# Gate and value projections: two sums of weight blocks formed by accumulating transfers from GpSimd's queue

## The chip, the core and the metric

One core of a Trainium2 chip runs the whole program. The metric is device time in microseconds, the median of the runs shown. Engines are named as in the profile: PE is TensorE (PEld its weight loads), DVE is VectorE, ACT is ScalarE, POOL is GpSimd, SP is SyncE, which issues nearly all transfers.

## The reference, cut to what matters

One layer of a hybrid trunk is followed by a gated feed-forward block. The part that the change touches is the pair of wide products `h @ w_gate` and `h @ w_val`: 512 tokens, 2048 inputs, 5504 outputs each, in float32.

```python
h = rmsnorm(x, norm_ffn_g[l])
gate = causal_dwconv(h @ w_gate[l], f_conv_w[l], f_conv_b[l])   # taps over 3 tokens
val = h @ w_val[l]
x = x + (jax.nn.gelu(gate) * val) @ w_down[l]
```

## The kernel before

Everything lies with channels on the 128 partitions and the 512 tokens along the row. The gate and value products ("gv") are 43 passes, of which each makes two 128-wide tiles of gate outputs or of value outputs in turn (the last pass takes one of each), and a pass is two stages, so there are 86 stages `s`, each for one half of the inputs. A stage uses a fast 2x2 block scheme with seven products in place of eight: from four weight blocks W0..W3 of 128x512 it needs seven operands, namely W1, W2, W3 and four sums. In the raw area of the stage, seven blocks of 512 columns, the transfer puts W0..W3 in blocks 0 to 3; `b_adds` then makes block 4 = W0+W1 and block 5 = W0+W2 in one DVE instruction of 1024 columns (L1147), block 6 = block 4 + W2 (L1148) and block 0 = block 6 + W3 (L1149). Blocks 4 and 5 are the sums that the change calls S1 and S3.

Each operand is split into a rounded part and its remainder so that three products give nearly full precision: `b_cast` copies all seven blocks (3584 columns) on ACT into the high area (L1153), `b_sub` subtracts that from the raw area on DVE into the low area (L1157), and `b_mm` (L208 to L210) runs 84 matmuls of 128x256 on PE, three for each of 28 weight tiles, the third of the three with the low part. There are two raw areas (`aR0`, `aR1`), two high and two low ones, used by even and odd stages.

The order on each engine is the order in which the loop writes the instructions. In step `s` it writes: the transfer for stage `s+2` (it goes into the raw area that `b_sub(s)` has read, so SP waits for that instruction), stores of finished hidden tiles to `hidd` (two of 256 KB in every fourth step), the cast of stage `s+1`; in even steps the six instructions of `b_post` on DVE, which empty the banks of the pass before (L1191 to L1196), and a scaling (gate, L1204) or product (value, L1226); then the subtraction of `s+1`, the 84 matmuls of `s`, the sums of `s+2`, and for gate the taps (L1218).

The first two stages are prepared during the last 16 products of the block before ("wm", loop over `m`): the transfer of stage 0 is written at m = 10, its sums at m = 12, its cast and the transfer of stage 1 at m = 14. In that loop GpSimd adds squares into `x2` (L1262), once for each m. In the gv stages GpSimd has nothing to do.

Of the kernel before, what the change touches and what calls it, by code (L numbers as in the profile page):

```python
# [14 lines left out]
MUL, ADD, SUB, MAX, MIN = ALU.mult, ALU.add, ALU.subtract, ALU.max, ALU.min  # L15

P = 128
T = 512
# [30 lines left out]
def f(ap):  # L49
    return ap.bitcast(F32)  # L50
# [3 lines left out]
def trunk(ctx: ExitStack, tc: tile.TileContext, A: dict, out: bass.AP):  # L54
    nc = tc.nc
    V, S, G, PE = nc.vector, nc.scalar, nc.gpsimd, nc.tensor
# [15 lines left out]
    def pair(i, dt):  # L72
        return sl.tile([P, 2 * T], dt, tag=f"p{i}", name=f"p{i}")

    def part(t, i, n=1):
        return t[:, i * T:(i + n) * T]
# [9 lines left out]
    def slot(dt=F32, name="s"):  # L86
        q = mosubs if name in ("MOh", "MOl") else () if name == "acc" else subs[dt]
        if q:
            t = q.popleft()
            owner[id(t)] = (q, t)  # L90
        else:
            i = free.popleft()
            cnt[0] += 1
            t = sl.tile([P, T], dt, tag=f"s{i}", name=f"{name}_{cnt[0]}")
            owner[id(t)] = (i, t)
        return t

    def drop(*ts):
        for t in ts:
            i = owner.pop(id(t))[0]  # L100
            if isinstance(i, int):
                free.append(i)
            else:
                i.append(t)

    def acc_ps(name):
        return ps.tile([P, T], F32, tag="acc", name=name, bufs=5)
# [22 lines left out]
    def vcol(n, i=0, w=1):  # L130
        c = VCOL[n] + i
        return vec[:, c:c + w]
# [79 lines left out]
    def dense(pt, nch, xh, xl):  # L212

        for c in range(nch):
            wh, wl = wget()
            for k in range(8):
                i = c * 8 + k
                w = slice(k * P, (k + 1) * P)
                mm3(pt, wh[:, w], wl[:, w], xh[i], xl[i], i == 0, i == nch * 8 - 1)
            if c < nch - 1:  # L220
                pump()
# [768 lines left out]
    for k in range(KT):  # L990
        if k < 2 or k % 2 == 0:
            wh, wl = ready.popleft()
        w = slice(0, T) if k < 2 else slice((k % 2) * T, (k % 2) * T + T)
# [4 lines left out]
        for j in range(4):  # L998
            if k < 14:
                mm3(upt[j], xh[k][:, j::4], xl[k][:, j::4], wh[:, w], wl[:, w], k == 0, False)  # L1000
            elif k == 15:
                for q in range(14, 16):
                    w = slice((q % 2) * T, (q % 2) * T + T)
# [24 lines left out]
    for c in range(8):  # L1028
        wh, wl = wget()
        for j in range(4):  # L1030
            for q in range(2):
                k = 2 * c + q
                w = slice(q * T, (q + 1) * T)
# [78 lines left out]
    RS = [aR0, aR1]  # L1112
# [6 lines left out]
    def t_build(kp):  # L1119

        x = (p1 if kp % 2 else p0).rearrange("p (b t) -> p b t", t=HT)
        v = p2.rearrange("p (b t) -> p b t", t=HT)
        V.tensor_tensor(out=v[:, 0:2], in0=x[:, 0:1].to_broadcast([P, 2, HT]), in1=x[:, 1:3], op=SUB)
        V.tensor_tensor(out=v[:, 2], in0=x[:, 2], in1=v[:, 0], op=SUB)
        V.tensor_tensor(out=v[:, 3], in0=x[:, 3], in1=v[:, 2], op=SUB)
        if kp % 2 == 0:
            TP["half"] = [slot(F32R, "T") for _ in range(2)]
            TS[kp // 4].extend(TP["half"])
        h, l = [t[:, kp % 2 * HT:kp % 2 * HT + HT] for t in TP["half"]]
        split(h, l, x[:, 1])  # L1130
        TP[kp, 1] = h, l
        for src, qs in ((x[:, 2:4], (6, 2)), (v[:, 0:2], (3, 4)), (v[:, 2:4], (5, 0))):
            h, l = slot(F32R, "T"), slot(F32R, "T")
            TS[kp // 4].extend([h, l])
            split(h, l, src.rearrange("p b t -> p (b t)"))
            for j, q in enumerate(qs):
                TP[kp, q] = [t[:, j * HT:j * HT + HT] for t in (h, l)]

    def b_dma(s):
        if s < NS:  # L1140
            nc.sync.dma_start(out=RS[s % 2][:, 0:4 * T], in_=A["wgv"][s // 2, s % 2])

    def b_adds(s):
        if s >= NS:
            return
        v = RS[s % 2].rearrange("p (b t) -> p b t", t=T)
        V.tensor_tensor(out=v[:, 4:6], in0=v[:, 0:1].to_broadcast([P, 2, T]), in1=v[:, 1:3], op=ADD)  # L1147
        V.tensor_tensor(out=v[:, 6], in0=v[:, 4], in1=v[:, 2], op=ADD)  # L1148
        V.tensor_tensor(out=v[:, 0], in0=v[:, 6], in1=v[:, 3], op=ADD)  # L1149

    def b_cast(s, lo=0, hi=7):
        if s < NS:
            S.copy(out=part(RH[s % 2], lo, hi - lo), in_=part(RS[s % 2], lo, hi - lo))  # L1153

    def b_sub(s, lo=0, hi=7):
        if s < NS:
            V.tensor_tensor(out=part(RL[s % 2], lo, hi - lo), in0=part(RS[s % 2], lo, hi - lo),  # L1157
                            in1=f(part(RH[s % 2], lo, hi - lo)), op=SUB)
# [73 lines left out]
    def put_out():  # L1232
        while stores:
            o, i_ = stores.popleft()
            nc.sync.dma_start(out=o, in_=i_)
# [3 lines left out]
    for m in range(16):  # L1239
        pt = acc_ps("wm")  # L1240
        dense(pt, 1, MOh, MOl)
        put_out()
        if m > 0:
            drop(acc[m - 1])
        V.tensor_tensor(out=acc[m], in0=acc[m], in1=pt, op=ADD)
        stores.append((x1d[m], acc[m]))
        if m == 10:
            b_dma(0)
        elif m == 12:
            b_adds(0)  # L1250
        elif m == 14:
            assert not raws
            b_cast(0)
            b_dma(1)
        x = p1 if m // 2 % 2 else p0
        S.activation(out=part(x, m % 2), in_=acc[m], func=AF.Copy, scale=vcol("g_ffn", m))
        if m == 0:
            S.activation(out=x2, in_=acc[m], func=AF.Square)
        else:
            sq = slot(name="sq")  # L1260
            S.activation(out=sq, in_=acc[m], func=AF.Square)
            G.tensor_tensor(out=x2, in0=x2, in1=sq, op=ADD)  # L1262
            drop(sq)
        if m == 14:
            b_sub(0, 1, 4)
        elif m % 2 and m < 15:
            t_build(m // 2)
    drop(*MOh, *MOl)
# [2 lines left out]
    put_out()  # L1271
    t_build(7)
    b_adds(1)
    US = slot(name="u")

# [63 lines left out]
    for s in range(NS + 1):  # L1339
# [4 lines left out]
        if s < NS - 2:  # L1344
            b_dma(s + 2)
# [14 lines left out]
        if s < NS:  # L1360
            b_mm(s)
        b_adds(s + 2)
        if even and gate:
            g_taps(k0, n)
# [29 lines left out]
    for k in range(KD):  # L1394
        d_dma(k + 2)
        d_split(k + 1)
        if k == 6:
# [4 lines left out]
            for i in (1, 2):  # L1402
                t = pair(i, F32R)
# [230 lines left out]
```

## Time and profile before

| | us |
|---|---|
| median of 3 runs (2117.73 to 2120.08) | 2118.34 |
| the profiled execution's own time | 2120.67 |
| its span | 2118.9 |
| gv stages, first matmul to last | 738.1 to 1624.3 |
| PE, DVE, ACT, POOL busy, share of the span | 98, 71, 38, 14% |

Busy time of PE is made of matmuls that overlap, so 98% doesn't say that none of them waited. A short wait between two matmuls is seen only in their start times: in the gv stages these lie 0.12 us apart where nothing holds PE.

### The profile page before, as it was taken

Reading aid. Unit: us, or ns where it says so; the run is one execution under the profiler, and the core shown is the slowest. Engines: PE = TensorE matmul, PEld = TensorE weight load, DVE = VectorE, ACT = ScalarE, POOL = GpSimd, SP = SyncE. Lnnn points to the kernel's source line nnn. Section 1 sums busy time; section 2 is a strip of 40 time slices with the busy share of each in tenths; the row PEclk is TensorE's granted clock in tenths of the full one; section 3 lists DMA queues with packets and bytes.
Section 4 is the critical chain, followed back from the end, with each engine's and each line's share of the span. In section 5 each row is a group of like instructions: output and inputs, shape, how many; then the busy total and the mean of one; then the engine's idle time right before and its main releaser. Section 6 shows DMA issues by size and latency. Waiting matters only on the chain.

```text
span 2118.9 us, 31328 instructions
## 1 busy us (share of the span) xinstructions
PE 2067.7 (98%) x12956; PEld 1881.7 (89%) x12956; DVE 1507.2 (71%) x2017; ACT 799.2 (38%) x946; POOL 290.0 (14%) x511
## 2 busy tenths in 40 slices
PE   8999989999999999999999999999999999999997
PEld 7887778888888799999999999999998888888887
DVE  7699996458655788989889898898886544222235
ACT  5244433345424543333443334333343432111124
POOL 4877660001101200000000000000000000000003
PEclk9999999999999989999999999999999999999999
DMA  4222113222333323333433333333332555333352
GB/s 172 83 73 76 63 53 110 82 87 80 115 139 115 136 103 119 111 110 114 135 110 110 120 120 119 120 110 111 118 131 90 188 174 190 110 110 113 119 199 80
DMA packets 75369, 244.73 MB, mean 115 GB/s; under 512 B 8397, under 2 KB 14029, under 8 KB 64217
## 3 DMA queue, kind: packets, MB, share of 16 engines
q1 hardware_dynamic: 75224, 242.72, 33.5%
q8 instruction: 101, 1.65, 0.3%
q14 instruction: 44, 0.35, 0.0%
HBM read 220.12 MB, written 22.57 MB: 115 GB/s over the span
## 4 chain that ended last, share of the span: by engine, by line
PE 80%; DVE 13%; POOL 2%; issue 2%; ACT 2%; DMA 1%; SPq 0%; DVEq 0%; ACTq 0%; POOLq 0%
PE gv L210 14%; PE gv L208 14%; PE gv L209 13%; PE down L209 7%; PE down L210 7%; PE down L208 7%; DVE a L116 2%; PE o L208 1%; PE ws L208 1%; PE ws L210 1%; PE o L210 1%; PE o L209 1%; PE ws L209 1%; PE v L208 1%; PE v L210 1%
## 5 line engine op out<-in xcount | busy, mean ns | idle before, releaser
L210 PE MATMUL gv<-T,a 128*128 128x256 f32 x2408 | 687.2, 285 | 4.4 <-DVE a L1157 4.4
L208 PE MATMUL gv<-T,a 128*128 128x256 f32 x2408 | 683.7, 284 | 4.0 <-ACT a L1153 4.0
L209 PE MATMUL gv<-T,a 128*128 128x256 f32 x2408 | 683.0, 284 | 0.0
L210 PEld LDWEIGHTS gv<-T,a 128*128 128x128 f32 x2408 | 463.9, 193 | 9.6 <-DVE a L1157 4.9
L208 PEld LDWEIGHTS gv<-T,a 128*128 128x128 f32 x2408 | 464.1, 193 | 4.5 <-ACT a L1153 4.5
L1153 ACT CAST a<-a 128x3584 fp32r<-128x3584 f32 x86 | 274.8, 3196 | 502.9 <-DVE a L1149 373.1
L209 PEld LDWEIGHTS gv<-T,a 128*128 128x128 f32 x2408 | 464.1, 193 | 0.0
L116 DVE TENSOR_TENSOR a<-a,a 128x1024 fp32r<-128x1024 f32 (+2 forms) x205 | 238.6, 1166 | 302.1 <-ACT a L115 301.1
L1157 DVE TENSOR_TENSOR a<-a,a 128x3584 fp32r<-128x3584 f32 (+2 forms) x88 | 336.2, 3822 | 82.7 <-ACT a L1153 82.6
L115 ACT CAST a<-a 128x1024 fp32r<-128x1024 f32 (+2 forms) x205 | 198.7, 973 | 379.6 <-PE down L209 296.1
L1486 POOL TENSOR_TENSOR c<-c,c 128x256 f32<-128x256 f32 x24 | 17.8, 741 | 1339.3 <-ACT c L1484 1338.4
L208 PE MATMUL down<-c,a 128*128 128x512 f32 x448 | 175.4, 392 | 4.0 <-ACT c L115 4.0
L210 PE MATMUL down<-c,a 128*128 128x512 f32 x448 | 175.0, 391 | 0.0
L209 PE MATMUL down<-c,a 128*128 128x512 f32 x416 | 162.9, 392 | 0.1
L1147 DVE TENSOR_TENSOR a<-a 128x1024 f32<-128x1024 f32 x86 | 104.8, 1219 | 0.0
L208 PEld LDWEIGHTS down<-c,a 128*128 128x128 f32 x448 | 84.6, 189 | 22.1 <-ACT c L115 4.4
L210 PEld LDWEIGHTS down<-c,a 128*128 128x128 f32 x448 | 84.7, 189 | 17.6
L209 PEld LDWEIGHTS down<-c,a 128*128 128x128 f32 x416 | 78.6, 189 | 16.9 <-DVE c L116 0.7
L209 PE MATMUL down<-a,a 128*128 128x512 f32 x176 | 68.5, 389 | 0.0
L208 PE MATMUL down<-a,a 128*128 128x512 f32 x176 | 68.5, 389 | 0.0
L1218 DVE SCALAR_TENSOR_TENSOR p<-p,vec,p 128x511 f32<-128x511 f32 x86 | 62.5, 748 | 2.5 <-ACT p L1211 0.9
L1149 DVE TENSOR_TENSOR a<-a 128x512 f32<-128x512 f32 x86 | 60.5, 703 | 2.9
(589 smaller groups left out, 3608.1 us busy)
## 6 DMA issues: line engine op xcount, KB each, us to landing
a<-in_wgv SPq DMA_DIRECT2D x86, 1024.0 KB, 4.8
a<-in_wdB SPq DMA_DIRECT2D x55, 512.0 KB, 3.4
a<-in_wdA SPq DMA_DIRECT2D x40, 320.0 KB, 3.2
hidd<-p SPq DMA_DIRECT2D x40, 256.0 KB, 6.2
a<-in_wxm SPq DMA_DIRECT2D x16, 512.0 KB, 3.3
a<-in_wv SPq DMA_DIRECT2D x16, 512.0 KB, 3.2
a<-in_wo SPq DMA_DIRECT2D x16, 512.0 KB, 3.2
a<-in_wouts SPq DMA_DIRECT2D x16, 512.0 KB, 3.5
```

The costliest lines, as they stand in the source:

```text
L115: S.copy(out=h, in_=src)
L116: V.tensor_tensor(out=l, in0=src, in1=f(h), op=SUB)
L208: PE.matmul(pt, lhsT=wh, rhs=xh, start=first, stop=False)
L209: PE.matmul(pt, lhsT=wh, rhs=xl, start=False, stop=False)
L210: PE.matmul(pt, lhsT=wl, rhs=xh, start=False, stop=last)
L1147: V.tensor_tensor(out=v[:, 4:6], in0=v[:, 0:1].to_broadcast([P, 2, T]), in1=v[:, 1:3], op=ADD)
L1149: V.tensor_tensor(out=v[:, 0], in0=v[:, 6], in1=v[:, 3], op=ADD)
L1153: S.copy(out=part(RH[s % 2], lo, hi - lo), in_=part(RS[s % 2], lo, hi - lo))
L1157: V.tensor_tensor(out=part(RL[s % 2], lo, hi - lo), in0=part(RS[s % 2], lo, hi - lo), in1=f(part(RH[s % 2], lo, hi - lo)), op=SUB)
L1218: V.scalar_tensor_tensor(out=y1[:, s:], in0=gs[:, 0:T - s], scalar=vcol("f_cw", 3 * (k0 + j) + 2 - s), in1=y1[:, s:], op0=MUL, op1=ADD)
L1486: G.tensor_tensor(out=x2, in0=x2, in1=sq[:, 0:HT], op=ADD)
```

## The change

The transfer of a stage becomes three. SP's first puts W0 twice, into blocks 4 and 5 (512 KB); its second puts W1..W3 into blocks 1 to 3 (768 KB); block 0 is no longer loaded. A transfer on GpSimd's queue then adds W1 and W2, read from HBM again (512 KB), onto blocks 4 and 5. The DVE instruction L1147 is gone from all 86 stages. In the loop over m the transfers of stage 1 are written after the first part of the subtraction of stage 0, in place of right after its cast.

```diff
     def b_dma(s):
         if s < NS:
-            nc.sync.dma_start(out=RS[s % 2][:, 0:4 * T], in_=A["wgv"][s // 2, s % 2])
+            r, w = RS[s % 2], A["wgv"][s // 2, s % 2]
+            v = r.rearrange("p (b t) -> p b t", t=T)
+            nc.sync.dma_start(out=v[:, 4:6], in_=w[:, 0:T].unsqueeze(1).to_broadcast([P, 2, T]))
+            nc.sync.dma_start(out=r[:, T:4 * T], in_=w[:, T:4 * T])
+            nc.gpsimd.dma_start(out=r[:, 4 * T:6 * T], in_=w[:, T:3 * T], accum_op=ADD)
 
     def b_adds(s):
...
-        V.tensor_tensor(out=v[:, 4:6], in0=v[:, 0:1].to_broadcast([P, 2, T]), in1=v[:, 1:3], op=ADD)
         V.tensor_tensor(out=v[:, 6], in0=v[:, 4], in1=v[:, 2], op=ADD)
         V.tensor_tensor(out=v[:, 0], in0=v[:, 6], in1=v[:, 3], op=ADD)
...
         elif m == 14:
             assert not raws
             b_cast(0)
-            b_dma(1)
...
         if m == 14:
             b_sub(0, 1, 4)
+            b_dma(1)
```

On DVE, a value step and the step after it, in the kernel before (`a_73` and `a_68` are the raw areas, `a_72`/`a_70` the high ones, `a_69`/`a_71` the low ones):

```order
L1226 TENSOR_TENSOR p_76<-p_76,p_75 128x1024
L1157 TENSOR_TENSOR a_71<-a_68,a_70 128x3584
L1147 TENSOR_TENSOR a_73<-a_73 128x1024
L1148 TENSOR_TENSOR a_73<-a_73 128x512
L1149 TENSOR_TENSOR a_73<-a_73 128x512
L1157 TENSOR_TENSOR a_69<-a_73,a_72 128x3584
```

The same place now; line numbers are three higher:

```order
L1229 TENSOR_TENSOR p_76<-p_76,p_75 128x1024
L1160 TENSOR_TENSOR a_71<-a_68,a_70 128x3584
L1151 TENSOR_TENSOR a_73<-a_73 128x512
L1152 TENSOR_TENSOR a_73<-a_73 128x512
L1160 TENSOR_TENSOR a_69<-a_73,a_72 128x3584
```

The instruction of 1024 columns between a subtraction and the two sums of 512 columns is gone; nothing else on DVE moved.

On GpSimd's queue, the end of the loop over m and the first gv stages, in the changed kernel, with the semaphores that each row waits for (DMAHW is a transfer from SP, DMASW one from GpSimd):

```order
L1264 TENSOR_TENSOR x_360_5404<-x_360_5404,sq_6038 128x512 [waits Activation_49,Pool_49]
L1145 DMA a_68<-in_wgv 128x1024 [waits DMAHW6_49,DMAHW2_49,DVE_49]
L1264 TENSOR_TENSOR x_360_5404<-x_360_5404,sq_6073 128x512 [waits Activation_49]
L1145 DMA a_73<-in_wgv 128x1024 [waits DMAHW6_49,DMASW0_49,DVE_49]
L1145 DMA a_68<-in_wgv 128x1024 [waits DMAHW0_49,DMASW1_49,DVE_49]
```

The accumulating transfer of stage 1 stands between the additions of squares of m = 14 and m = 15, and from there on the queue holds only such transfers, each of which waits for SP's transfer of W0 into the same area.

## Rows read from the trace of the kernel before

**Rows 1.** Page part 4: chain of waits, share of the span by engine.

```profile
PE 80%; DVE 13%; POOL 2%; issue 2%; ACT 2%; DMA 1%; SPq 0%; DVEq 0%; ACTq 0%; POOLq 0%
```

**Rows 2.** Busy time of each engine in four stretches; first row names the columns.

```profile
core 0: us, PE busy (x) PEld busy (x) DVE busy (x) ACT busy (x) POOL busy (x), PEclk, DMA share, GB/s
746.00:786.00 40.00, 35.22 (x270) 34.84 (x269) 33.09 (x46) 15.45 (x9) 0.00 (x0) 0.87 0.28 103
786.00:900.00 114.00, 114.00 (x952) 114.00 (x951) 100.38 (x95) 45.64 (x28) 0.00 (x0) 1.00 0.35 116
1100.00:1300.00 200.00, 200.00 (x1653) 198.66 (x1652) 176.66 (x165) 76.96 (x45) 0.00 (x0) 1.00 0.35 114
1207.50:1214.00 6.50, 6.50 (x55) 6.49 (x55) 3.04 (x4) 3.46 (x2) 0.00 (x0) 1.00 0.79 241
```

**Rows 3.** Timeline of PE: start, us, engine, line, operation, at two stage starts.

```profile
922.40 0.28 PE L209 MATMUL gv<-T,a 128*128 128x256 f32 x1
922.62 0.39 PE L210 MATMUL gv<-T,a 128*128 128x256 f32 x1
...
1207.30 0.28 PE L209 MATMUL gv<-T,a 128*128 128x256 f32 x1
1207.51 0.39 PE L210 MATMUL gv<-T,a 128*128 128x256 f32 x1
```

**Rows 4.** Timeline of DVE and ACT over two stages; idle before in brackets.

```profile
1203.58 3.88 DVE L1157 TENSOR_TENSOR a<-a,a 128x3584 fp32r<-128x3584 f32 x1
1207.38 1.22 DVE L1147 TENSOR_TENSOR a<-a 128x1024 f32<-128x1024 f32 x1
...
1210.21 3.20 ACT L1153 CAST a<-a 128x3584 fp32r<-128x3584 f32 x1 [7.36 <-DVE a L1149]
...
1213.44 3.90 DVE L1157 TENSOR_TENSOR a<-a,a 128x3584 fp32r<-128x3584 f32 x1 [3.39 <-ACT a L1153]
1217.25 1.22 DVE L1147 TENSOR_TENSOR a<-a 128x1024 f32<-128x1024 f32 x1
1218.50 0.69 DVE L1148 TENSOR_TENSOR a<-a 128x512 f32<-128x512 f32 x1
...
1223.92 3.88 DVE L1157 TENSOR_TENSOR a<-a,a 128x3584 fp32r<-128x3584 f32 x1
```

**Rows 5.** Timeline of DVE: the subtractions of stages 3 and 85.

```profile
776.24 3.88 DVE L1157 TENSOR_TENSOR a<-a,a 128x3584 fp32r<-128x3584 f32 x1
...
1610.53 3.88 DVE L1157 TENSOR_TENSOR a<-a,a 128x3584 fp32r<-128x3584 f32 x1
```

**Rows 6.** Groups of instructions: the one that the change removes.

```profile
L1147 DVE TENSOR_TENSOR a<-a 128x1024 f32<-128x1024 f32 x86 | 104.8, 1219 | 0.0
```

**Rows 7.** Timeline at the start of the gv stages: POOL, DVE, ACT, PE.

```profile
739.30 1.64 POOL L1262 TENSOR_TENSOR x<-x,sq 128x512 f32<-128x512 f32 x1 [5.76 <-ACT sq L1261]
...
747.83 1.22 DVE L1147 TENSOR_TENSOR a<-a 128x1024 f32<-128x1024 f32 x1
...
750.54 3.18 ACT L1153 CAST a<-a 128x3584 fp32r<-128x3584 f32 x1 [4.06 <-DVE a L1149]
...
757.70 0.58 PE L210 MATMUL gv<-T,a 128*128 128x256 f32 x1 [3.13 <-DVE a L1157]
```

**Rows 8.** Transfers: issues (KB, median us to landing), and those of L1141 alone.

```profile
a<-in_wgv SPq DMA_DIRECT2D x86, 1024.0 KB, 4.8
...
a<-in_wxm SPq DMA_DIRECT2D x16, 512.0 KB, 3.3
...
L1141 SPq DMA_DIRECT2D a<-in_wgv x86: 327/332/425, 706.9 to 1594.1; - x86
...
DMA to landing us min/median/max: 4.6/4.8/7.2
```

**Rows 9.** Timeline: a GpSimd and a DVE instruction side by side.

```profile
726.95 1.59 POOL L1262 TENSOR_TENSOR x<-x,sq 128x512 f32<-128x512 f32 x1 [6.04 <-ACT sq L1261]
...
727.43 1.67 DVE L1149 TENSOR_TENSOR a<-a 128x512 f32<-128x512 f32 x1
```

## The prediction

> **What bounds the kernel now.** I read the chain of waits first: PE holds 80% of it and DVE 13% [rows 1], so a gain has to shorten PE's own time or a wait of PE. The stretches come next [rows 2]. From 786 to 900 us PE runs 952 matmuls in 114.0 us, 0.1197 us each; from 1100 to 1300 us it runs 1653 in 200.0 us, 0.1210 us each, at the same granted clock of 1.00. Something takes about 1% from PE in the later stretch although its busy time reads 200.00 of 200.00. DVE is busy 88% in both, which alone would not make it a suspect.
>
> The starts of the matmuls show where the 1% lies [rows 3]. Matmuls start 0.12 us apart, but at 1207.30 the next start comes 0.21 later, and the same stands at 922.40 (0.22). The late one is an L210, the first in its stage to use the low part, and the subtraction that makes this part ends at 1203.58 + 3.88 = 1207.46 [rows 4], 0.05 before it. PE waits there for DVE. This happens once in two stages, 36 times from 902 to 1614 us; before 902 PE still has work in hand.
>
> Why DVE is late is seen by following one round of two stages [rows 4]. Subtraction to 1207.46; sums from 1207.38; cast on ACT from 1210.21, 3.20 long, while DVE waits 3.39; subtraction to 1217.34; sums again from 1217.25; post-processing of a pass; subtraction to 1227.80. Each step waits for the one before it, so this is a closed round: 1227.80 - 1207.46 = 20.34 us. From the subtraction of stage 3 (ends 780.12) to that of stage 85 (ends 1614.41) [rows 5] it takes 834.29 us for 41 rounds, 20.35 each. PE needs 168 x 0.12 = 20.16. So DVE's round, idle time included, sets the pace, and PE merely lives off its backlog until 902.
>
> **The change part by part.** Removed: 86 instructions of 1.219 us on DVE [rows 6]. Two of them lie in each round, in front of a cast or of the post-processing, so the round falls by 2 x 1.22, to about 17.9 us. That is below PE's 20.16, so PE sets the pace and only its waits are won: from 902 to 1614 us there are 35 rounds, each 20.35 - 20.16 = 0.19 too long, together 6.7 us. Of the 104.8 us that DVE sheds, the rest becomes idle time of DVE.
>
> At the start of the stages the sum of stage 1 (747.83) is followed by its cast (750.54) and by PE, which had waited 3.13 us for the low part when it went on at 757.70 [rows 7]. There 1.22 us comes off if the transfers are in. The sum of stage 0, at m = 12, has no such wait behind it that I would count.
>
> Added: the chain of transfers. Now SP issues one transfer when the subtraction has freed the raw area, and it lands 4.6 to 7.2 us later, 4.8 in the median [rows 8]; DVE takes the data up at the next subtraction's end, about 10 us later. After the change the sums wait for W0, then GpSimd, then the accumulation. Call the whole latency L, from the end of the subtraction of a stage to the moment when blocks 4 and 5 are complete. No row shows a transfer from GpSimd's queue or an accumulating one, so each term has bounds:
> - W0 twice, 512 KB: between 3.3 (a 512 KB load) and 4.8 (1 MB) [rows 8]. The value is 3.3, since the 768 KB behind it on the same queue come later.
> - GpSimd's share, making the transfer ready: between 0.33, which an issue takes on SP [rows 8], and 1.6, the longest of its tensor instructions shown beside a DVE one [rows 9]. I take 1.2, nearer to the latter since those are the rows of the engine that does it; 0.1 is added for the semaphore.
> - The accumulation, 512 KB read from HBM and 512 KB read back from the area: between 3.3 and 7.2 [rows 8]. I take 4.8, that of 1 MB.
>
> L = 3.3 + 0.1 + 1.2 + 4.8 = 9.4 us, with ends 3.3 + 0.3 + 3.3 = 6.9 and 4.8 + 1.6 + 7.2 = 13.6. In every fourth step two stores of 256 KB share the engines: between 1207.5 and 1214 the transfers keep them 79% busy [rows 2], and landing grows by up to 7.2 - 4.6 = 2.6. They always hit the odd stages, every second one of these; with half of 2.6 as the value, the odd stages' mean is 9.4 + 1.3 / 2 = 10.0.
>
> The accumulation sums two inputs on the way, and the Trainium skill (Collectives: The Full Stack, The bandwidth ceiling: the fold count and why AG ≠ RS ≠ AR) says that such a reduction runs at half of a copy's rate because it needs two source reads. No run here shows one; the row of 1 MB that I take for 512 KB agrees with it, and at a copy's rate L would be 7.9.
>
> What L may be: the same raw area is used every second stage, so a second round exists. Subtraction, L, two sums, post-processing, next subtraction. The part without L is from 1218.50 (the first sum that stays) to 1227.80, 9.3 us [rows 4]. This round is L + 9.3, and it costs nothing while it is below 20.16, that is L up to 10.9; single stages may be later, since DVE, no longer the limit, finishes some 2 us before PE needs it (cast 3.2 and subtraction 3.9 after a stage's start leave 2.9 of 10.1). With 10.0 the cover is 0.9 us. If it is gone, each microsecond costs 41 us in all. That the bytes of a stage rise from 1 MB to 1.75 MB costs nothing by itself: the engines are 35% busy [rows 2].
>
> The moved transfer of stage 1: on SP nothing changes, and on GpSimd the accumulation stands behind the addition of squares at 739.30 [rows 7]; ready at 740.9, it should land 6.0 later, near 747, when DVE comes to it at 747.8. The cover is under a microsecond and what it hides is worth 1.2.
>
> Sum against the profiled execution: 2120.67 - 6.7 - 1.2 = 2112.8; the median is 2.3 lower than that execution, so 2110.4.
>
> **The rivals.**
> 1. The transfers are late: L passes 10.9 in the odd stages, and their round replaces the one of DVE. It decides from there; at 11.05 the old 20.35 is reached, and each further microsecond adds 41 us. With 12 the round is 21.3 and the time 2118.3 + 41 x 0.95 = 2157; with 13.6 it is 22.9 and 2223. For it speaks that three steps in series replace one, and that 7.2 has been seen for one of them; against it that 10.0 leaves cover, and that traffic is light between the stages.
> 2. DVE and GpSimd hold each other up. The rows show a DVE sum of 0.69 stretched to 1.67 beside a GpSimd instruction [rows 9]. If making a transfer ready has to wait for the DVE instruction that runs, half of a subtraction of 3.9, or 1.9 us, is added to L: 11.9, a round of 21.2, and 2153. Against it: in one stage of two DVE stands idle for the cast when W0 lands (1207.46 + 3.3 = 1210.8, idle to 1213.44) [rows 4]. The Trainium skill (SBUF — State Buffer, SBUF: two separate sides) warns of this: a transfer from GpSimd's queue starves while DVE runs an instruction in a mode that uses both ports, because its descriptors can't be written. For an instruction with two inputs in SBUF, as all of these are, it limits the lock to GpSimd instructions that read SBUF; no run here shows which of the two holds for this transfer.
> 3. The 0.2 us at the start of every second stage is not a wait for DVE but PE's own, or comes back in another form (a late landing near L = 11). Then only the 1.2 us at the start is won: 2117. Against it: there is none of it before 902 us, while PE has a backlog.
>
> **How the numbers follow.** A difference of 0.2% (4.2 us) is about what a measurement can tell from none. Forecast, PE sets the pace: 0.58, 2110.4. Rival 1: 0.21. Rival 2: 0.08. Rival 3: 0.13. So faster 0.58, same 0.13, slower 0.29. Below the forecast lies the granted clock at the start, 0.87 of full speed from 746 to 786 us [rows 2], between its two levels of 1.2 and 2.4 GHz after PE had stood waiting; if a shorter wait kept it up, at most 0.13 x 40 = 5.2 us would come off, so the low end is 2105. The high end has to take in a third of rivals 1 and 2, up to a mean L of 11.6: 2118.3 + 41 x 0.55 = 2141. The forecast's own range is 2105 to 2114.
>
> **What would show it.** Right: matmuls 0.12 us apart at all stage starts, 168 in 20.16 us; DVE idle in front of its casts' ends and not in front of the first sum; the last gv matmul 7 to 8 us earlier. The accumulation must land within 10.9 us of the subtraction's end. Wrong: DVE waiting in front of the sum that reads block 4, with the transfer as releaser, in odd stages above all; rounds of more than 20.35; DVE instructions that are longer than before; GpSimd's transfer instruction longer than 1.6 us. The forecast falls if the accumulation lands later than 7 us after its issue.

## The result and the profile after

The changed kernel takes 2200.71 us in the median (4 runs, 2195.13 to 2204.26) against 2119.21 us of the kernel before beside it: 1.0384 times as long, interval 1.0364 to 1.0404, or 81 us slower. The profiled execution has a span of 2196.4 us, 77.5 more than before.

First the page of the changed kernel: the chain of waits by engine, three groups of instructions (busy us, mean ns | idle us of the engine just before them, and what ended it), and the issues of transfers (KB, median us to landing).

```profile
PE 43%; DVE 28%; DMA 24%; issue 4%; ACT 2%; SPq 0%; POOLq 0%; DVEq 0%; POOL 0%; ACTq 0%
...
L210 PE MATMUL gv<-T,a 128*128 128x256 f32 x2408 | 697.9, 290 | 61.5 <-DVE a L1160 61.5
...
L1145 POOL DMA_DIRECT2D a<-in_wgv x86 | 74.7, 869 | 868.1 <-DMA a<-in_wgv 588.7
...
L1151 DVE TENSOR_TENSOR a<-a 128x512 f32<-128x512 f32 x86 | 59.4, 691 | 182.0 <-DMA a<-in_wgv 182.0
...
a<-in_wgv SPq DMA_DIRECT2D x86, 768.0 KB, 8.2
a<-in_wgv SPq DMA_DIRECT2D x86, 512.0 KB, 6.5
a<-in_wgv POOLq DMA_DIRECT2D x86, 512.0 KB, 5.5
```

PE's share of the chain fell from 80% [rows 1] to 43%, and transfers have 24% of it where they had 1%. DVE, which before had no idle time in front of its first sum [rows 6], now stands idle 182.0 us in front of it (L1151), for GpSimd's transfer: 155.5 of them in odd stages and 26.4 in even ones. GpSimd in its turn waits for SP's transfer of W0, which lands 6.5 us after its issue in the median.

Two rounds of the same raw area in the changed kernel, those of the odd stages 43 and 45, from the timelines (start, us, engine, line; the idle time before in brackets). The transfer at 1208.07 is that of the even stage 44, into the other area:

```profile
1195.02 3.89 DVE L1160 TENSOR_TENSOR a<-a,a 128x3584 fp32r<-128x3584 f32 x1
...
1198.93 0.38 SPq L1143 DMA_DIRECT2D a<-in_wgv  x1
...
1199.41 0.41 SPq L1144 DMA_DIRECT2D a<-in_wgv  x1
1199.86 1.40 SPq L1238 DMA_DIRECT2D hidd<-p  x2
...
1206.88 0.86 POOL L1145 DMA_DIRECT2D a<-in_wgv  x1 [12.25 <-DMA a<-in_wgv]
1208.07 0.38 SPq L1143 DMA_DIRECT2D a<-in_wgv  x1
...
1213.28 0.69 DVE L1151 TENSOR_TENSOR a<-a 128x512 f32<-128x512 f32 x1 [5.23 <-DMA a<-in_wgv]
...
1218.70 3.89 DVE L1160 TENSOR_TENSOR a<-a,a 128x3584 fp32r<-128x3584 f32 x1
1222.61 0.38 SPq L1143 DMA_DIRECT2D a<-in_wgv  x1
...
1229.18 0.88 POOL L1145 DMA_DIRECT2D a<-in_wgv  x1 [11.38 <-DMA a<-in_wgv]
...
1234.45 0.69 DVE L1151 TENSOR_TENSOR a<-a 128x512 f32<-128x512 f32 x1 [3.27 <-DMA a<-in_wgv]
...
1239.87 3.88 DVE L1160 TENSOR_TENSOR a<-a,a 128x3584 fp32r<-128x3584 f32 x1
```

This is the round of the first rival. A subtraction ends at 1198.91 and frees the area; W0 of stage 43 is issued at 1198.93, W1 to W3 at 1199.41 and two stores behind them; GpSimd starts at 1206.88, DVE's first sum at 1213.28, 14.37 us after the subtraction; the next subtraction in this area ends at 1222.59: 23.68 us. In the round of stage 45, without stores, GpSimd starts at 1229.18, the sum at 1234.45, 11.86 us after the subtraction, and the next subtraction ends at 1243.75: 21.16 us. Over the stages 8 to 83 the sum begins 13.10 us after the subtraction in odd stages and 13.68 in even ones, and the round is 22.4 us; from stage 3 (ends 776.39) to stage 85 (1691.65) it is 22.32 in the mean, against 20.35 before [rows 5]. 41 rounds of 1.97 more are +80.9 us. Stage 3 was done 3.7 us sooner than before. Together that is +77.2, against 77.5 between the spans.

The stretches of [rows 2], for the changed kernel:

```profile
786.00:900.00 114.00, 108.20 (x885) 107.59 (x884) 77.08 (x73) 38.33 (x21) 8.67 (x10) 0.99 0.71 181
1100.00:1300.00 200.00, 188.70 (x1527) 187.67 (x1526) 139.96 (x133) 69.91 (x39) 15.60 (x18) 0.97 0.69 178
```

PE makes 1527 matmuls in 200 us where it made 1653; the transfer engines are 69% busy where they were 35%, though the bytes in the stretch rose only from 114 to 178 GB/s.

### The profile page after: what moved, and what is told of

Read it like the earlier page. It is cut to its first block, busy times and chain, and to the rows that moved or that the text cites. A ratio compares the mean times of both kernels' runs of the same rounds, so it can differ in the third digit from the quotient of the medians.

```text
span 2196.4 us, 31723 instructions
## 1 busy us (share of the span) xinstructions
PE 2090.1 (95%) x12956; PEld 1904.4 (87%) x12956; DVE 1406.5 (64%) x1931; ACT 800.2 (36%) x946; POOL 364.9 (17%) x597
## 3 DMA queue, kind: packets, MB, share of 16 engines
q0 software_dynamic: 12384, 45.09, 12.3%
## 4 chain that ended last, share of the span: by engine, by line
PE 43%; DVE 28%; DMA 24%; issue 4%; ACT 2%; SPq 0%; POOLq 0%; DVEq 0%; POOL 0%; ACTq 0%
DMA a<-in_wgv 23%; DVE a L1160 8%; PE down L209 7%; PE down L210 7%; PE down L208 7%; DVE a L116 2%; PE o L208 1%; DVE a L1151 1%; PE ws L208 1%; PE o L210 1%; PE ws L210 1%; PE ws L209 1%; PE o L209 1%; DVE p L1199 1%; DVE p L1229 1%
## 5 line engine op out<-in xcount | busy, mean ns | idle before, releaser
L210 PE MATMUL gv<-T,a 128*128 128x256 f32 x2408 | 697.9, 290 | 61.5 <-DVE a L1160 61.5
L208 PE MATMUL gv<-T,a 128*128 128x256 f32 x2408 | 694.6, 288 | 1.8 <-ACT a L1156 1.8
L209 PE MATMUL gv<-T,a 128*128 128x256 f32 x2408 | 694.0, 288 | 0.0
L210 PEld LDWEIGHTS gv<-T,a 128*128 128x128 f32 x2408 | 474.7, 197 | 67.2 <-DVE a L1160 67.0
L208 PEld LDWEIGHTS gv<-T,a 128*128 128x128 f32 x2408 | 474.7, 197 | 2.4 <-ACT a L1156 2.3
L209 PEld LDWEIGHTS gv<-T,a 128*128 128x128 f32 x2408 | 474.4, 197 | 0.0
L1145 POOL DMA_DIRECT2D a<-in_wgv x86 | 74.7, 869 | 868.1 <-DMA a<-in_wgv 588.7
L1151 DVE TENSOR_TENSOR a<-a 128x512 f32<-128x512 f32 x86 | 59.4, 691 | 182.0 <-DMA a<-in_wgv 182.0
```

The source lines that it names most:

```text
L208: PE.matmul(pt, lhsT=wh, rhs=xh, start=first, stop=False)
L209: PE.matmul(pt, lhsT=wh, rhs=xl, start=False, stop=False)
L210: PE.matmul(pt, lhsT=wl, rhs=xh, start=False, stop=last)
L1145: nc.gpsimd.dma_start(out=r[:, 4 * T:6 * T], in_=w[:, T:3 * T], accum_op=ADD)
```

## The experiments

Theories: (1) DVE's round was the limit, and its removal is worth some 8 us when the data are in time; (2) a second round, subtraction, transfers, sums, subtraction, is as long as L + 9.3 us and takes over when L passes 10.9; and for what makes L long: (A) what SP issues behind W0, (B) the short rows of W0's transfer, (C) the accumulation of the stage before. The rival to (1) is that the short delays belong to PE. In the figures below "start" is GpSimd's transfer and "L" DVE's first sum, both counted from the end of the subtraction that frees the area, means of the stages 8 to 83 given as odd / even. In odd stages the changed kernel's sum starts when the transfer lands (5.94 and 5.92 us after GpSimd's start), so this L is the prediction's; in even ones DVE comes to it a little later (5.70 against 5.47). Where one run is given, these figures are those of its one execution, and a time that differs by less than some 9 us, the spread of the changed kernel's four runs, says little by itself.

**The sums left out, plain loads in time** (edit to the kernel before):

```diff
+            nc.sync.dma_start(out=RS[s % 2][:, 4 * T:6 * T], in_=A["wgv"][s // 2, s % 2][:, T:3 * T])
...
-        V.tensor_tensor(out=v[:, 4:6], in0=v[:, 0:1].to_broadcast([P, 2, T]), in1=v[:, 1:3], op=ADD)
```

> The kernel before without the DVE sum L1147 and without any transfer from GpSimd: blocks 4 and 5 are filled by a second transfer of SP's (512 KB, the raw blocks W1 and W2, so the sums S1 and S3 are left out of what is computed). It measures what the removal of the DVE instruction is worth by itself when the data come in time (1.5 MB on one queue should land some 6 to 7 us after the subtraction, against the 10 us that DVE needs). First theory, DVE's round of 20.35 us was the limit and PE's 20.16 takes over: 7 to 9 us less than before, about 2111, and matmuls 0.12 us apart at every stage start. Rival, the delay of 0.2 us at the start of every second stage is PE's own: only the 1.2 us at the start is won, about 2118, and the delays stay.

Measured: 2109.46 us against 2117.85, ratio 0.9963 (0.9949 to 0.9976). The same two stretches of this kernel:

```profile
786.00:900.00 114.00, 114.00 (x953) 114.00 (x952) 87.66 (x87) 46.55 (x26) 0.00 (x0) 1.00 0.50 175
1100.00:1300.00 200.00, 200.00 (x1669) 200.00 (x1668) 154.02 (x149) 78.37 (x46) 0.00 (x0) 1.00 0.48 169
```

1669 matmuls in 200 us are 0.1198 us each, the pace that PE had before only until 900 us. So the delays were waits for DVE, and theory (1) holds with its size: 8 us. The rival to it falls. It also shows that 1.5 MB in a stage, on SP's queue alone, does no harm. The first of the two transfers, 1 MB in rows of 8 KB, lands in the 4.8 us that it took alone [rows 8], although 512 KB are issued right behind it:

```profile
a<-in_wgv SPq DMA_DIRECT2D x86, 1024.0 KB, 4.8
a<-in_wgv SPq DMA_DIRECT2D x86, 512.0 KB, 5.7
```

**W1 to W3 left out after the second stage** (edit to the changed kernel):

```diff
+            if s < 2:
-            nc.sync.dma_start(out=r[:, T:4 * T], in_=w[:, T:4 * T])
+                nc.sync.dma_start(out=r[:, T:4 * T], in_=w[:, T:4 * T])
```

> The changed kernel, but W1 to W3 are loaded for the first two stages only, so SP's second transfer (768 KB) is missing from the other 84 and blocks 1 to 3 hold old weights. Theory A, W0's transfer lands 6.5 to 8 us after the subtraction because the 768 KB issued 0.4 us behind it share the engines with it: W0 lands after 3.3 to 4, the accumulation's start falls from 7.6 to about 4, L to 10 and the round to PE's 20.16; time about 2112. Theory B, the 2 KB rows of W0's transfer are slow by themselves: nothing changes, GpSimd starts at 6.6 or later, about 2190. Theory C, the accumulation of the stage before is what W0's transfer meets: the transfers that took 8 us fall to about 6.5 and no further, about 2165.

Measured: 2107.51 us, one run, against 2117.85. Start 4.74 / 4.47, L 10.08 / 10.47, round 20.16. Issues of this kernel, and its first sum with DVE's idle time:

```profile
a<-in_wgv SPq DMA_DIRECT2D x86, 512.0 KB, 3.8
a<-in_wgv POOLq DMA_DIRECT2D x86, 512.0 KB, 5.4
```

```profile
L1152 DVE TENSOR_TENSOR a<-a 128x512 f32<-128x512 f32 x86 | 59.1, 688 | 20.9 <-DMA a<-in_wgv 20.5
```

W0 lands in 3.8 where it took 6.5, and PE sets the pace again, although each stage still accumulates. This is A as it was written, and C by itself is not enough. DVE waits 20.9 us in front of the first sum where it waited 182.0, so L is here mostly the time at which DVE itself comes to the sum.

**W0 with long rows** (the first transfer reads 4 KB rows, W0 and W1, so the sums have other terms):

```diff
-            nc.sync.dma_start(out=v[:, 4:6], in_=w[:, 0:T].unsqueeze(1).to_broadcast([P, 2, T]))
+            nc.sync.dma_start(out=r[:, 4 * T:6 * T], in_=w[:, 0:2 * T])
```

> The changed kernel, but SP's first transfer reads 512 KB as rows of 4 KB (W0 and W1 side by side) in place of W0 twice in rows of 2 KB, so blocks 4 and 5 start from other weights; bytes, order and waits are the same. Theory B, the form of the rows is what makes this transfer slow: GpSimd starts 4 us after the subtraction, L falls from 13.4 to about 10, time near 2115. Theories A and C, what runs beside it is what counts: no change beyond 0.5 us in L, 2180 to 2205.

Measured: 2123.81 us, one run. Start 5.17 / 4.80, L 11.21 / 11.74, round 20.50. Issues:

```profile
a<-in_wgv SPq DMA_DIRECT2D x86, 768.0 KB, 5.9
a<-in_wgv SPq DMA_DIRECT2D x86, 512.0 KB, 4.2
a<-in_wgv POOLq DMA_DIRECT2D x86, 512.0 KB, 5.4
```

With the 768 KB still behind it, the same number of bytes lands in 4.2. The time lies between the two that were expected, nearer to theory B. So A alone is wrong as well: it takes both, the form of W0's transfer (short rows, one block read twice; this run changes the two together) and the transfer behind it. Alone, that form costs 0.5 (3.8 against 3.3 of another load of 512 KB in [rows 8]); in front of 768 KB it costs 2.3 (6.5 against 4.2). The packet records of the changed kernel show the two transfers in work at the same time: in odd stages without stores the first packet of the 768 KB starts 3.0 us after W0's issue, when 59 of W0's 256 packets have not started yet (medians).

**A plain copy in place of the accumulation** (the sums are left out):

```diff
-            nc.gpsimd.dma_start(out=r[:, 4 * T:6 * T], in_=w[:, T:3 * T], accum_op=ADD)
+            nc.gpsimd.dma_start(out=r[:, 4 * T:6 * T], in_=w[:, T:3 * T])
```

> The changed kernel, but GpSimd's transfer is a plain copy of W1 and W2 over blocks 4 and 5, with the same waits, so the sums are left out of what is computed. It measures what accumulating costs against copying. Theory A: the start of GpSimd's transfer stays at 7 to 8 us after the subtraction, and only its own 5.7 us falls, to about 4, so L is 11 to 12, the round 20.5 to 21.2, time 2125 to 2155. Theory C, the accumulation's load on the engines is what slows W0's transfer of the next stage: both fall, L below 10.5, time near 2112.

Measured: 2140.05 us, one run. Start 7.31 / 6.97, L 11.71 / 12.11, round 21.0. Queues of this kernel (packets, MB, share of 16 engines) and its issues, and then the queue of GpSimd in the changed kernel:

```profile
q0 software_dynamic: 12384, 45.09, 6.1%
...
a<-in_wgv SPq DMA_DIRECT2D x86, 768.0 KB, 7.6
a<-in_wgv SPq DMA_DIRECT2D x86, 512.0 KB, 6.2
a<-in_wgv POOLq DMA_DIRECT2D x86, 512.0 KB, 3.9
```

```profile
q0 software_dynamic: 12384, 45.09, 12.3%
```

The same packets and bytes hold the engines twice as long when they accumulate, 12.3% of 2196 us against 6.1% of 2138, and land 1.6 us later. Of the 1.6, 0.34 is GpSimd's own instruction, from whose start the landing is counted: 0.87 us in the changed kernel, 0.53 here. W0's start in odd stages is what it was (7.31 against 7.16), as A has it; in even stages it is 1.0 less than the 7.98 of the changed kernel, as C would have it. The odd stage's accumulation lands 3.7 us after the even stage's W0 is issued in the changed kernel, and 2.7 here, so the two do meet; that the 1.0 comes from this alone is not shown.

**W1 alone behind W0** (256 KB in place of 768, blocks 2 and 3 keep old weights):

```diff
-            nc.sync.dma_start(out=r[:, T:4 * T], in_=w[:, T:4 * T])
+            n = 4 if s < 2 else 2
+            nc.sync.dma_start(out=r[:, T:n * T], in_=w[:, T:n * T])
```

> The changed kernel, but from the third stage on SP's second transfer brings W1 alone (256 KB in rows of 2 KB) and blocks 2 and 3 hold old weights. So far W0 lands in 3.8 us with nothing behind it and in 6.5 with 768 KB behind it. If it shares the engines with what is behind it in proportion to the bytes, it lands at about 3.8 + 2.7/3 = 4.7, GpSimd starts at 5.3 to 5.6, L is 11.2 and the round 20.5: 2120 to 2128. If any second transfer on the queue delays it by the same amount, it lands at 6.5 and the time is 2180 to 2200. If short transfers slip behind it unseen, it lands at 3.8 to 4.0 and the time is PE's, 2106 to 2112.

Measured: 2109.22 us, one run. Start 5.59 / 5.23, L 10.91 / 11.48, round 20.21. Issues:

```profile
a<-in_wgv SPq DMA_DIRECT2D x86, 512.0 KB, 4.5
...
a<-in_wgv SPq DMA_DIRECT2D x84, 256.0 KB, 4.8
```

W0 lands in 4.5, near the 4.7 of a share by bytes, and GpSimd starts when that theory has it, though the time itself is one that was expected for another (W0 at 3.8 to 4.0). W1 alone also comes in shorter rows than the 768 KB, so a share by bytes is not singled out. The time was put too high by some 10 us, since L came out 0.3 shorter and so right at the point from which the second round costs: 10.91 + 9.3 = 20.21, measured 20.21.

**W0 in two transfers of 256 KB**, and **W1 to W3 in three with short rows** (two kernels that compute all):

```diff
-            nc.sync.dma_start(out=v[:, 4:6], in_=w[:, 0:T].unsqueeze(1).to_broadcast([P, 2, T]))
+            for b in (4, 5):
+                nc.sync.dma_start(out=v[:, b], in_=w[:, 0:T])
```

> The changed kernel with W0 loaded by two transfers of 256 KB, one for block 4 and one for block 5, in place of one that repeats it; rows of 2 KB and the bytes stay. If the rows of 2 KB make W0 slow, nothing changes but one more issue of 0.4 us on SP: GpSimd starts 7 to 8.5 us after the subtraction, 2195 to 2215. If it is the repeated form of the one transfer, W0 lands in 4.2 as with rows of 4 KB, and the time is 2115 to 2130.

```diff
-            nc.sync.dma_start(out=r[:, T:4 * T], in_=w[:, T:4 * T])
+            for b in (1, 2, 3):
+                nc.sync.dma_start(out=v[:, b], in_=w[:, b * T:b * T + T])
```

> The changed kernel with W1 to W3 loaded by three transfers with rows of 2 KB in place of one with rows of 6 KB; the bytes stay, W0's transfer is untouched. If the engines share row by row, so that the long rows behind W0 hold up its short ones, W0 now lands earlier, at 4 to 5, L falls to 10.5 to 11, time 2110 to 2130, though W1 to W3 land later. If short rows are slow whatever comes behind, W0 lands at 6.5 as before, W1 to W3 later than 8.2, and the time is 2195 to 2230.

Measured: 2157.55 and 2158.91 us, one run each. Two transfers: start 6.01 / 6.40, L 12.04 / 12.68, round 21.34. Three short ones: start 6.50 / 7.03, L 12.21 / 12.82, round 21.5, and W0 lands in 5.8. In the first W0's transfers land in 4.7 each. Each kernel gains about 42 us, half of what was lost, and none of the four expectations was met: neither the repeated form, nor the rows of 2 KB, nor the length of what comes behind is the cause by itself. How the engines choose between two transfers of one queue stays open; the way round it that follows doesn't depend on it.

**The subtraction in two pieces** (edit to the changed kernel):

```diff
-        b_sub(s + 1)
+        b_sub(s + 1, 4, 7)
+        b_sub(s + 1, 0, 4)
```

> The changed kernel with the subtraction in two pieces, blocks 4 to 6 first (1.8 us) and blocks 0 to 3 after (2.1 us). SP's transfer of W0 into blocks 4 and 5 then waits for the first piece alone and is issued some 2.1 us earlier, and the 768 KB of W1 to W3 come 2.1 us behind it in place of 0.4. Theory, the latency of the chain is all that is wrong: W0 lands in 3.8 to 4.5 as in the run without W1 to W3, so GpSimd starts about 2.7 after the end of the subtraction in place of 7.2 to 8.0, the sums' data are there by 8 to 9, the round is PE's 20.16, and the time 2108 to 2114, below the kernel before. Rival, the load on the engines from 1.75 MB in each stage is what costs: the accumulation beside the 768 KB takes 7 us and more, L stays above 10.9, and the time is 2125 to 2160.

Measured: 2108.84 us (6 runs) against 2116.98, ratio 0.9956 (0.9943 to 0.9968), so 8 us faster than the kernel before and some 92 faster than the changed one. Its issues, its first sum with DVE's idle time, and a stretch:

```profile
a<-in_wgv SPq DMA_DIRECT2D x86, 768.0 KB, 5.2
a<-in_wgv SPq DMA_DIRECT2D x86, 512.0 KB, 3.7
a<-in_wgv POOLq DMA_DIRECT2D x86, 512.0 KB, 7.0
```

```profile
L1151 DVE TENSOR_TENSOR a<-a 128x512 f32<-128x512 f32 x86 | 59.0, 686 | 13.2 <-DMA a<-in_wgv 13.1
```

```profile
1100.00:1300.00 200.00, 200.00 (x1669) 200.00 (x1668) 155.74 (x168) 79.97 (x45) 17.39 (x20) 1.00 0.73 196
```

W0 is issued 2.2 us before the subtraction ends, and W1 to W3 follow 2.2 us behind it in place of 0.4; it lands in 3.7, and GpSimd starts 2.24 / 2.53 after the subtraction's end. Of the 4.9 us that the odd stages' start gains, 2.2 are the earlier issue and the rest is W0's shorter landing (3.7 for 6.5). The accumulation, now beside the 768 KB, takes longer (7.0 against 5.5), as the rival to this run had it; but L is 9.90 / 10.44, the round 20.16, and DVE's 182.0 us of waiting have become 13.1. The engines are 73% busy, more than in the changed kernel, and 1669 matmuls fit into 200 us. So the load of a whole stage was not the trouble; the time at which the chain began, and what was issued right behind its first transfer, were.

**The control: the kernel before with the same cut and nothing else.** The edit is the same.

> The kernel before with nothing but the subtraction cut in two pieces, the control for the kernel that beat both. Theory: the cut by itself frees nothing that anyone waits for, it only adds 0.07 us to a subtraction of 3.89 in DVE's round, two in each: 20.35 + 0.14 = 20.49, 41 rounds, so 5 to 6 us slower than the kernel before, and all of the gain of the other kernel comes from the sum that DVE no longer makes. Rival: the cut helps by itself, since PE or the transfers are released earlier: 2 us or more faster.

Measured: 2121.65 us (9 runs) against 2117.34, ratio 1.0023 (1.0013 to 1.0033), 4.9 us slower by the ratio, a little less than the 5 to 6 that were expected.

```profile
1100.00:1300.00 200.00, 199.31 (x1642) 197.29 (x1641) 176.70 (x184) 76.98 (x45) 0.00 (x0) 1.00 0.35 114
```

0.07 us in each subtraction lengthen DVE's round to 20.49, as expected, and 1642 matmuls fit in place of 1653. The gain of the kernel above over the kernel before is that of the missing sum.

## Why the prediction was wrong, step by step

- **DVE's round bounds the kernel, and PE's 20.16 would take over:** right. The run without the sums gave -8 us (0.37%, interval 0.24 to 0.51) where 7.9 was worked out. The control confirms it from the other side: 0.14 us more in a round cost 4.9 us.
- **The start of the stages:** the 1.2 us was right for the sum of stage 1, and the sum of stage 0, counted at nothing, gave 0.9 more. The subtraction of stage 1 ends at 754.56 against 757.64; 0.9 of these 3.1 us were there at the first transfer of the gv weights already, which the change doesn't touch. From that transfer on it is 48.6 us against 50.8, and 50.8 in the control too, which still has L1147. The sum of stage 0 had met GpSimd's instruction of [rows 9] there, a DVE instruction of 1.67 in place of 0.69; whether the 0.9 is this stretch or that sum's own 1.22 us is not told apart. The moved transfer of stage 1 was in time: DVE did not wait for it.
- **A second round of L + 9.3, free up to L = 10.9:** right, to a tenth of a microsecond. Since L is counted to DVE's first sum, what is tested is that the rest of the round stays 9.3 and that PE's 20.16 holds below L = 10.9. With L of the odd stages:

| kernel | L | L + 9.3 | round |
|---|---|---|---|
| changed | 13.10 | 22.4 | 22.4 |
| W1 to W3 with short rows | 12.21 | 21.5 | 21.5 |
| W0 in two transfers | 12.04 | 21.3 | 21.3 |
| plain copy | 11.71 | 21.0 | 21.0 |
| W0 with long rows | 11.21 | 20.5 | 20.5 |
| W1 alone | 10.91 | 20.2 | 20.2 |
| W1 to W3 left out | 10.08 | 19.4 | 20.16 (PE) |
| two pieces | 9.90 | 19.2 | 20.16 (PE) |

- **L = 10.0:** wrong, 13.1, and this decides the case. The term that failed is the first, W0's transfer. It was put at 3.3, the row of a 512 KB load, "since the 768 KB behind it on the same queue come later". They come 0.4 us later and it lands in 6.5; its bounds were 3.3 and 4.8, so it lies outside both. The rows used stand for transfers with rows of 4 KB or more and mostly with nothing behind them. Alone it does land in 3.8. The 0.1 for the semaphore, for which no row was named, was 0.6: from W0's landing to GpSimd's start it takes 0.62 us in the median. Measured, the sum is 6.5 + 0.6 + 5.9 = 13.0 where 3.3 + 0.1 + 6.0, and 0.6 for the stores, had been added up.
- **GpSimd's share and the accumulation, 1.2 + 4.8 = 6.0:** right as a sum, in part by luck: GpSimd's instruction takes 0.87, and from its start to DVE's sum it is 5.94 / 5.70 us, so one term was too long and the other too short by about 0.3. The half rate that the Trainium skill states for a reduction (Collectives: The Full Stack, The bandwidth ceiling: the fold count and why AG ≠ RS ≠ AR) stands there for ReduceScatter between cores; for this transfer the trace shows the same factor: 12.3% of the engines against 6.1%.
- **The stores cost 1.3 in every second odd stage, 0.65 in the mean of the odd ones:** right in kind, too small. In the odd stages with stores (43 in the rows above) L is 14.13 in the mean, in those without 12.06, so the stores cost 2.1 there and 1.0 in the mean: 0.9 in GpSimd's start (7.62 against 6.70), the rest between that start and the sum. Without stores the start is still 3.3 later than the 3.4 of the prediction's sum. The even stages, which have no stores, start later still (7.98): their W0 is issued while the accumulation of the odd stage still runs, at 1208.07 in the rows above, with GpSimd's transfer issued at 1206.88. With a plain copy there, the even start fell by 1.0.
- **The sign "the accumulation lands later than 7 us after its issue":** it watched the wrong transfer. In the changed kernel the accumulation landed in 5.5 and the forecast fell; with the subtraction in two pieces it took 7.0 and the time was the one forecast.
- **Rival 1 (late transfers):** this is what happened, at 0.21. Its price was right: 41 x (22.4 - 20.35) = 84 us, measured 81. The bounds of L had been worked out to 13.6, or 2223 us; the range was cut at a mean L of 11.6, which left out the upper half of a rival none of whose transfers had been seen in a trace in the form and company that they would have.
- **Rival 2 (DVE and GpSimd hold each other up):** no sign of it. In the changed kernel GpSimd's transfer instructions and DVE's subtractions last (ns, least, median, most):

```profile
L1145 POOL DMA_DIRECT2D a<-in_wgv x86: 862/865/1019, 713.1 to 1677.1; - x86
...
L1160 DVE TENSOR_TENSOR a<-a,a x88: 1758/3887/3895, 736.2 to 1687.8; 128x3584 fp32r<-128x3584 f32 x85, 128x1536 fp32r<-128x1536 f32 x2, 128x512 fp32r<-128x512 f32 x1
```

  The subtraction takes what it took [rows 4], and GpSimd's instruction hardly varies whatever DVE does beside it: 46 of them lie wholly within a subtraction and take 0.87 us like the rest. The 0.62 us from W0's landing to its start are the same with a subtraction running all that time and without. The lock of which the Trainium skill warns (SBUF — State Buffer, SBUF: two separate sides) doesn't show beside these DVE instructions, which have two inputs; what it says of one-input modes no run here tests.
- **Rival 3 (PE's own delays):** refuted by the run without the sums.

## What to carry to other kernels

An engine that is 88% busy can be the limit when its instructions and its waits close a ring; look for the period of the ring in the start times, not for busy shares. When work moves from an engine to transfers, write down the ring that the transfers close, from the read that frees the buffer to the next such read, and what its slack is; then make the chain begin earlier (free first the part of the buffer that the chain needs, here by cutting one instruction in two) before giving the idea up. A landing time read from a trace belongs to its row length and to what was issued around it: here the row used said 3.3 us, and with short rows and another transfer right behind it was 6.5, so the bounds of such a term should reach to twice the row. A mean load of the engines (35% here) says nothing about the moment when two transfers start together.

## What the runs showed of the hardware

- A transfer of 512 KB in rows of 2 KB, one block read twice, landed in 3.8 us alone, in 4.5 with 256 KB issued 0.4 us behind it on the same queue, in 5.8 with 768 KB in three transfers of such rows behind it, and in 6.5 with 768 KB in one transfer of rows of 6 KB. With rows of 4 KB it took 4.2 with those same 768 KB behind it, and 1 MB in rows of 8 KB took 4.8 with and without 512 KB behind it. Why the short rows are slowed so much more is open.
- An accumulating transfer into SBUF held the 16 engines twice as long as a plain copy of the same bytes (12.3 against 6.1%) and landed after 5.5 us against 3.9; beside 768 KB of loads it took 7.0. GpSimd's instruction that issues it took 0.87 us, that of the plain copy 0.53.
- PE's granted clock fell at times in the changed kernel: after a wait of 3.26 us its matmuls were at first 0.12 and then 0.21 us apart, and from 1224.5 to 1226 the granted clock was 0.50, the lower of its two levels (1.2 of 2.4 GHz). Over 1100 to 1300 us it was 0.97 in the mean, where it was 1.00 before. Timeline of PE there, and the stretch:

```profile
1222.64 0.39 PE L210 MATMUL gv<-T,a 128*128 128x256 f32 x1 [3.26 <-DVE a L1160]
1222.86 0.28 PE L208 MATMUL gv<-T,a 128*128 128x256 f32 x1
1222.98 0.28 PE L209 MATMUL gv<-T,a 128*128 128x256 f32 x1
...
1224.56 0.41 PE L208 MATMUL gv<-T,a 128*128 128x256 f32 x1
1224.77 0.41 PE L209 MATMUL gv<-T,a 128*128 128x256 f32 x1
```

```profile
1224.50:1226.00 1.50, 1.50 (x9) 1.50 (x8) 1.47 (x3) 1.50 (x1) 0.00 (x0) 0.50 0.66 153
```

  It cost nothing more that shows: PE was waiting in each round anyway, and the rounds are L + 9.3.
